# A two-layer HGRN2 and Fourier mixer block on one Trainium2 core: token mixtures rebuilt later, two heads projected plainly, sums moved to GpSimd

## The chip, the cores and the metric

The program runs on 1 core of one Trainium2 chip. The metric is device microseconds of one execution, taken as the median of several runs. The kernel before has 1232.58 us (three runs: 1232.63, 1232.58 and 1231.08). The engines are named as in the profile: PE multiplies matrices (PEld loads its weights), DVE is VectorE, ACT is ScalarE, POOL is GpSimd, and SP issues the DMAs.

## What is computed

Two layers work on 512 latent tokens of width 1024, in float32; 256 context tokens are a prefix of layer 0. Cut to what matters:

```
layer 0: h = rms_norm(x) * (1 + scale) + shift      # scale, shift, gate: adaLN of c and c_ctx
         p = h @ hg_w_in                            # 5 streams: q, f1, f2, v, z; 16 heads of 128
         f = lb + (1 - lb) * sigmoid(p[1:3])        # two gates, forward and backward scan
         o = scan_forward(q, 1 - f1, v) + scan_backward(q, 1 - f2, v)
         x = x + gate * ((rms_norm(o) * silu(z)) @ hg_w_out)
layer 1: u, z = split(h1 @ ft_w_in);  y = real(fft2(u))
         x = x + gate * ((y * silu(z)) @ ft_w_out)
out:     rms_norm(x)
```

The context tokens need the gates f1, f2 and v only (they give the state from which the latent scans start). So q and z are products over 512 tokens, f1, f2 and v over 768.

## The kernel before

Every float32 product is made from halves. `split` (lines 57 to 59) rounds a tile to a high part on ACT (`wh`) and takes the remainder on DVE (`wl`), and `mm3` (lines 102 to 105) adds three matmuls: high by high, low by high, high by low. The normalized tokens stand transposed in `hlh` and `hll`, high and low parts of [128, 8, 768].

**The start** (lines 347 to 428) has an order written out by hand for PE, ACT and DVE. For each of eight blocks `d` of the model width, PE makes adaLN's row for the block (`rp`, line 225) and transposes the latent tokens (`tp`, line 244); ACT copies the row out (`row`, line 227); PE turns it into columns (`mp`, line 233); DVE makes `acol` and `bcol` from them; `modulate` (from line 246) writes `hlh` on ACT and `hll` on DVE. The products of head 0 (`first`) for block d - 2 lie between. The same is then done for the context tokens (`e` = 1), in a second loop over `d`, after their sums of squares (`square`) and `normalize`.

**The seven-product trick.** From head 1 on, the two gate streams of a head are not made as two full products but from seven products of quarter-size blocks (`px`, 84 matmuls of 384 columns), in the manner of Strassen and Winograd. For this the weights of the two streams are folded (`fold_piece`, four sums of 128x512 a head, on DVE, lines 297 to 302: tile `wr`), each of the seven results is split (`wp`), and four of the seven products use token mixtures `mix` in place of tokens. `mixes` (line 261) makes the mixtures during the start: for one block it takes four sums or differences on POOL in place in `xs` (lines 273 to 276), and splits the four results into `mix`. It is called once a block for the latent tokens at d = 4 to 7, and for two blocks at a time for the context tokens at d = 5 and 7. The results of the products are combined by additions of 128x384 on DVE or POOL (line 574).

**The stage of the heads** is one generator, `projections`: a pair of heads is head 2p, the V product of the pair (`vps`, 144 matmuls of 256 columns), and head 2p + 1. At each of its yields, `advance` takes one step of the oldest scan, so PE goes back and forth between projections and scans. A scan takes seven levels; at each, PE multiplies `gp` (line 678), DVE updates `z` in two instructions (line 686) and puts `gp` into `am` under a mask (line 705), and ACT gathers `kk` from `z` (line 644) for the next level's `gp`. Behind the levels come `ktp`, `sp`, the states `st` (DVE, line 731), `op`, its squares `os` (ACT, line 744), `rstd_o` (POOL, lines 187 and 188), `os` scaled (line 748), and `otp`. At the same yields `ada_rest` (line 440) steps through the rest of adaLN: 32 tiles `ar` of 512 KB are loaded one at a time into one buffer and added up in `acc` under a scalar (DVE, line 463). Outside the start, a scheduler sets the order of each engine's instructions when the kernel is built; on the chip each engine then keeps that order.

**Weights.** `specs` lists the weight tiles in the order of use. `loaded(n)` issues the loads (SP, three raw buffers `wr`), `halves(n)` folds and splits, and `get(n)` decides how far ahead the splits are asked for:

```
        def get(self, n):
            self.halves(n + 3 if n in pieces and pieces[n] < 4 else n + 1)
            self.loaded(n + 3)
            return self.parts[n]
```

Behind the heads come the output product of layer 0 (`o0a`), layer 1 and the output; none of this is touched.

Of the kernel before, what the change touches and what calls it, by code (L numbers as in the profile page):

```python
# [19 lines left out]
TC = 256  # L20
# [12 lines left out]
def hgrn_fourier_kernel(ctx: ExitStack, tc: tile.TileContext, a):  # L33
# [14 lines left out]
    def psP(name):  # L48
        return psum("P", 4, name)
# [7 lines left out]
    def split(hi, lo, src):  # L57
        s.activation(hi, src, AF.Copy)  # L58
        v.tensor_tensor(out=lo, in0=src, in1=hi.bitcast(F32), op=ALU.subtract)  # L59

    class Weights:
# [33 lines left out]
                self.parts.append((hi, lo))  # L95

        def get(self, n):
            self.halves(n + 3 if n in pieces and pieces[n] < 4 else n + 1)
            self.loaded(n + 3)
            return self.parts[n]  # L100

# [103 lines left out]
    def square(n):  # L205
        if n < 2 or n == NT:
            for b in range(2):
                junk[b] = p0.tile([P, D], F32, tag=f"junk{b}", name=f"junk{n}_{b}")
        if n % 2:
            v.scalar_tensor_tensor(out=junk[1], in0=xs[:, n, :], scalar=1.0, in1=xs[:, n, :], op0=ALU.mult, op1=ALU.mult,  # L210
                                   accum_out=ss[:, n:n + 1])
        else:
            s.activation(junk[0], xs[:, n, :], AF.Square, accum_out=ss[:, n:n + 1])
# [44 lines left out]
        v.tensor_tensor(out=tl[d].rearrange("p (n c) -> p n c", c=P), in0=h32,  # L258
                        in1=th[d].bitcast(F32).rearrange("p (n c) -> p n c", c=P), op=ALU.subtract)

    def mixes(k0, k1, e):
        m, n0 = ((2, 0), (1, NT))[e]
        xt = xs.rearrange("p n (h k c) -> p h k n c", h=2, c=P)

        def part(kh, half, k):
            return xt[:, kh, k, n0 + half:n0 + half + 2 * m - 1:2, :]

        for t in range(4):
            if mix[t] is None:
                mix[t] = [ph.tile([P, KT // 2, N // 2], F32R, tag=f"t{2 * t + b}", name=f"mix{t}_{b}") for b in range(2)]  # L270
        for k in range(k0, k1):
            b11, b12, b21, b22 = (part(kh, half, k) for kh in range(2) for half in range(2))
            g.tensor_tensor(out=b22, in0=b22, in1=b12, op=ALU.subtract)
            g.tensor_tensor(out=b12, in0=b12, in1=b11, op=ALU.subtract)
            g.tensor_tensor(out=b11, in0=b22, in1=b11, op=ALU.add)
            g.tensor_tensor(out=b21, in0=b21, in1=b11, op=ALU.subtract)
            for t, src in ((2, b22), (0, b12), (1, b11), (3, b21)):
                c = slice(0, 2 * P) if e == 0 else slice(2 * P, 3 * P)
                hi, lo = (mix[t][b][:, k, c].rearrange("p (n c) -> p n c", c=P) for b in range(2))
                split(hi, lo, src)  # L280


    specs = []
    at = {}
# [6 lines left out]
    def fold_piece(w, j):  # L291
        p = pieces[j]
        w.loaded(j - p + 1)
        f1, f2 = w.raw[j - p], w.raw[j - p + 1]
        a11, a12, a21, a22 = f1[:, :4], f1[:, 4:], f2[:, :4], f2[:, 4:]
        if p == 2:
            v.tensor_tensor(out=a21, in0=a21, in1=a22, op=ALU.add)
            v.tensor_tensor(out=a11, in0=a21, in1=a11, op=ALU.subtract)
        elif p == 4:
            v.tensor_tensor(out=a21, in0=a22, in1=a11, op=ALU.subtract)  # L300
        elif p == 5:
            v.tensor_tensor(out=a12, in0=a12, in1=a11, op=ALU.subtract)
        return (a11, a12, a11, a21, a21, a12, a22)[p]

    def head_specs(i):
        if i == 0:
            for st in (1, 2):
                spec(("w", i, st), a["hg_w"][i, st], [P, KT, P])
        else:
            for p in range(7):  # L310
# [43 lines left out]
    with tc.manual_schedule(engines={mybir.EngineType.PE, mybir.EngineType.Activation, mybir.EngineType.DVE}):  # L354
# [14 lines left out]
        W.loaded(2)  # L369
        for d in range(5, KT):  # L370
            ada_load(d)
        for n in range(NTC):
            nc.sync.dma_start(out=xs[:, NT + n, :], in_=a["ctx"][n * P:(n + 1) * P, :])
        W.loaded(3)
        mraw = p0.tile([P, 5, P], F32, name="mraw")
        nc.sync.dma_start(out=mraw, in_=a["masks"][:, :5, :])
        keep_warm(24, "warm1")
# [7 lines left out]
        for d in range(KT):  # L385
            if d > 0:
                ada_mm(d)
            if d == 5:
                lower_bounds()
            turn(d, 0)  # L390
            if d == 0:
                keep_warm(4, "warm3")
            for j, k in todo.get(d, [(j, d - 2) for j in range(3)] if d > 3 else []):
                product(j, k)
            if d == KT - 1:
                for n in range(NT, NT + NTC):
                    square(n)
            ada_cols(d)
            modulate(d, 0)
            if d < 3:  # L400
                W.halves(d)
            if d >= KT // 2:
                mixes(d - 4, d - 3, 0)
        W.halves(3)
        for j in range(3):
            product(j, KT - 2)
        for n in range(NT, NT + NTC):
# [13 lines left out]
        for d in range(KT):  # L421
            modulate(d, 1)
            product(3, d)
            if d + 2 < KT:
                turn(d + 2, 1)
            if d in (5, 7):
                mixes(d - 5, d - 3, 1)
    st_start.close()

    grow = [pd.tile([1, D], F32, name=f"grow{j}") for j in range(2)]  # L430
# [5 lines left out]

    st_hgrn = ExitStack()
    sp = st_hgrn.enter_context(tc.tile_pool(name="sp", bufs=1))

    def ada_rest():  # L440
        todo = [(j, k) for j in range(4) for k in range(KT)]
# [10 lines left out]
        for j in (0, 1, 2, 3):  # L452
# [4 lines left out]
            for k in range(KT):  # L457
                yield
                raw = raws[j * KT + k]
                if k == 0 and j in (1, 2):  # L460
                    v.tensor_scalar(out=acc, in0=raw, scalar1=scol[:, 0, k:k + 1], scalar2=None, op0=ALU.mult)
                else:
                    v.scalar_tensor_tensor(out=acc, in0=raw, scalar=scol[:, 0, k:k + 1], in1=acc,
                                           op0=ALU.mult, op1=ALU.add)
                fetch()
            yield
            if j in (0, 3):
# [45 lines left out]
    def proj(i):  # L513
# [17 lines left out]
        if i == 0:  # L531
# [61 lines left out]
        s.activation(ff[:, 0, :], ff[:, 0, :], AF.Sigmoid)  # L593
        gate(2)
        yield None
        for st, dst in ((0, q), (3, zs)):
            wh, wl = W.get(at["w", i, st])
            pl = psP(f"pq{i}_{st}")
            yield from lat_proj(pl, wh, wl, hlh[:, :, :T], hll[:, :, :T])
            silu(pl, dst)  # L600
            if st == 0:
                yield None
            else:
                yield scan(i, ff, z4, q, zs)
# [543 lines left out]
```

## Time and profile before

| what | value |
|---|---|
| median of three runs | 1232.58 us |
| the profiled execution | 1230.89 us, span 1229.1 us |
| PE busy | 1182.0 us (96%), 7497 matmuls |
| DVE, ACT, POOL busy | 880.9 (72%), 600.6 (49%), 104.4 us (8%) |
| DMA | 126.29 MB, mean 103 GB/s |
| PE's idle time by stage | 24.5 us in the first 93 us, 22.5 us in the 1136 us after |

The page gives, for each engine, the time in which it was busy and how many instructions it ran. Views of the trace give the same by stretch (busy time of each engine between two times, and the clock that PE was granted), by group of instructions (count, busy time, mean duration, and the idle time just before them with what ended it), as a timeline, as a list of who waited for whom, and as the chain of work that ended last. PE's durations overlap, as matmuls are pipelined: how fast it works is read from start to start.

### The profile page before, as it was taken

Reading aid. Unit: us, or ns where it says so; the run is one execution under the profiler, and the core shown is the slowest. Engines: PE = TensorE matmul, PEld = TensorE weight load, DVE = VectorE, ACT = ScalarE, POOL = GpSimd, SP = SyncE. Lnnn points to the kernel's source line nnn. Section 1 sums busy time; section 2 is a strip of 40 time slices with the busy share of each in tenths; the row PEclk is TensorE's granted clock in tenths of the full one; section 3 lists DMA queues with packets and bytes.
Section 4 is the critical chain, followed back from the end, with each engine's and each line's share of the span. In section 5 each row is a group of like instructions: output and inputs, shape, how many; then the busy total and the mean of one; then the engine's idle time right before and its main releaser. Section 6 shows DMA issues by size and latency. Waiting matters only on the chain.

```text
span 1229.1 us, 19234 instructions
## 1 busy us (share of the span) xinstructions
PE 1182.0 (96%) x7497; PEld 1054.5 (86%) x7497; DVE 880.9 (72%) x1492; ACT 600.6 (49%) x1205; POOL 104.4 (8%) x138
## 2 busy tenths in 40 slices
PE   7779999999999999999999999999999999999997
PEld 5559889988988988998898999898888998888885
DVE  5479886786897787788568668759666856658554
ACT  4356563664555465456365455456557533333322
POOL 2330100100110011010010010010010000000000
PEclk9979999999999999999999999999999999999999
DMA  9312430220531431232022022117546313333221
GB/s 353 142 37 88 143 104 27 78 87 26 162 121 44 140 127 52 79 128 88 25 78 85 28 78 69 35 53 246 182 143 201 105 52 114 113 118 120 86 86 69
DMA packets 39585, 126.29 MB, mean 103 GB/s; under 512 B 4537, under 2 KB 8130, under 8 KB 39494
## 3 DMA queue, kind: packets, MB, share of 16 engines
q1 hardware_dynamic: 39494, 125.06, 30.0%
q8 instruction: 59, 0.97, 0.3%
q14 instruction: 32, 0.26, 0.1%
HBM read 119.52 MB, written 5.51 MB: 102 GB/s over the span
## 4 chain that ended last, share of the span: by engine, by line
PE 72%; DVE 12%; ACT 8%; POOL 3%; issue 3%; DMA 2%; SPq 0%; DVEq 0%; POOLq 0%; ACTq 0%
PE gp L678 5%; DVE z L686 4%; PE px L103 4%; PE px L104 4%; PE px L105 3%; PE pq L105 3%; PE pq L104 3%; PE pq L103 3%; PE vps L103 3%; PE vps L105 3%; PE vps L104 3%; PE o0a L105 2%; PE o0a L103 2%; PE o0a L104 2%; PE o1a L103 2%
## 5 line engine op out<-in xcount | busy, mean ns | idle before, releaser
L58 ACT ACTIVATE wh<-wr 128x1024 fp32r<-128x1024 f32 x110 | 116.3, 1057 | 153.7 <-issue 53.4
L686 DVE TENSOR_TENSOR z<-z,tt 128x512 f32<-128x512 f32 x192 | 130.3, 721 | 69.5 <-PE gp L678 67.9
L59 DVE TENSOR_TENSOR wl<-wr,wh 128x1024 fp32r<-128x1024 f32 x110 | 134.1, 1219 | 33.3 <-ACT wh L58 33.1
L103 PE MATMUL vps<-wh,hlh 128*128 128x256 f32 x384 | 112.8, 294 | 0.5 <-ACT ff L533 0.5
L678 PE MATMUL gp<-z,kk 128*128 128x128 f32 x768 | 107.7, 283 | 5.7 <-ACT kk L644 4.9
L678 PEld LDWEIGHTS gp<-z,kk 128*128 128x128 f32 x768 | 95.9, 192 | 18.8 <-ACT kk L644 18.0
L644 ACT ACTIVATE kk<-z 128x512 f32<-128x512 f32 x96 | 61.5, 640 | 100.0 <-DVE z L686 96.3
L105 PE MATMUL vps<-wh,hll 128*128 128x256 f32 x384 | 109.9, 286 | 0.0
L104 PE MATMUL vps<-wl,hlh 128*128 128x256 f32 x384 | 108.9, 284 | 0.0
L58 ACT ACTIVATE wp<-wr 128x512 fp32r<-128x512 f32 x105 | 65.0, 627 | 82.4 <-PE pq L104 73.5
L105 PE MATMUL pq<-hlh,wl 128*128 128x512 f32 x240 | 95.6, 398 | 0.0
L103 PE MATMUL pq<-hlh,wh 128*128 128x512 f32 x240 | 95.4, 397 | 0.0
L104 PE MATMUL pq<-hll,wh 128*128 128x512 f32 x240 | 94.4, 393 | 0.0
L574 POOL TENSOR_TENSOR ff<-u,c 128x384 f32<-128x384 f32 x30 | 45.4, 1515 | 492.5 <-ACT c L570 408.9
L59 DVE TENSOR_TENSOR wp<-wr,wp 128x512 fp32r<-128x512 f32 x105 | 71.0, 686 | 20.1 <-ACT wp L58 19.8
L103 PE MATMUL px<-mix,wp 128*128 128x384 f32 x240 | 84.4, 352 | 0.0
L104 PE MATMUL px<-mix,wp 128*128 128x384 f32 x240 | 82.1, 342 | 0.0
L105 PE MATMUL px<-mix,wp 128*128 128x384 f32 x240 | 81.3, 339 | 0.0
L103 PEld LDWEIGHTS vps<-wh,hlh 128*128 128x128 f32 x384 | 73.7, 192 | 2.8 <-issue 2.1
L104 PEld LDWEIGHTS vps<-wl,hlh 128*128 128x128 f32 x384 | 73.8, 192 | 0.7 <-issue 0.5
L105 PEld LDWEIGHTS vps<-wh,hll 128*128 128x128 f32 x384 | 73.8, 192 | 0.6 <-issue 0.6
L103 PE MATMUL px<-hlh,wp 128*128 128x384 f32 x180 | 62.3, 346 | 0.0
(286 smaller groups left out, 3095.1 us busy)
## 6 DMA issues: line engine op xcount, KB each, us to landing
wr<-hg_w SPq DMA_DIRECT2D x64, 512.0 KB, 3.6
ar<-ada_r SPq DMA_DIRECT2D x32, 512.0 KB, 3.5
wr<-ft_w SPq DMA_DIRECT2D x32, 512.0 KB, 4.1
wr<-hg_wout SPq DMA_DIRECT2D x29, 512.0 KB, 3.8
wa<-ada_a SPq DMA_DIRECT2D x16, 512.0 KB, 11.2
wr<-hg_v SPq DMA_DIRECT2D x16, 512.0 KB, 4.6
wr<-ft_wout SPq DMA_DIRECT2D x16, 512.0 KB, 3.5
yd<-y SPq DMA_DIRECT2D x13, 256.0 KB, 2.8
```

The costliest lines, as they stand in the source:

```text
L58: s.activation(hi, src, AF.Copy)
L59: v.tensor_tensor(out=lo, in0=src, in1=hi.bitcast(F32), op=ALU.subtract)
L103: pe.matmul(out, lh, rh, start=first, stop=False)
L104: pe.matmul(out, lh, rl, start=False, stop=False)
L105: pe.matmul(out, ll, rh, start=False, stop=last)
L574: eng.tensor_tensor(out=dst, in0=x, in1=y, op=ALU.add)
L644: s.activation(view(kk, 0, [[2 * h, T // (2 * h)], [h, 2], [1, h]]), view(z4, 2 * T, [[2 * h, T // (2 * h)], [T + h, 2], [1, h]]), AF.Copy)
L678: pe.matmul(gp[:, n * P:(n + 1) * P], kk[:, n * P:(n + 1) * P], view(z4, n * P, dims), start=True, stop=True)
L686: v.tensor_tensor(out=za, in0=za, in1=ta, op=ALU.mult)
```

## The change

1. `mixes` leaves the start. It becomes a generator that is stepped at each yield of `projections`, behind `advance`: for each of four blocks it adds the high and low parts back to whole tokens (two POOL additions of 128x768 from `hlh` and `hll` into `whole`), takes the four sums or differences on POOL over all 768 tokens (128x384 each), and splits the four results. The two `whole` tiles take the buffers of `ar` and `acc`, one of each.
2. Head 1 is projected plainly, as head 0's weights are: its two gate streams are 2 x 24 matmuls of 512 columns (latent) and 2 x 24 of 256 columns (context), in place of 84 of 384 columns. The pieces begin with head 2.
3. `fold_piece`'s four sums of 128x512 a head go from DVE to POOL (now for 14 heads, 56 sums, instead of 15 heads).
4. `ada_rest`: the multiplication by the scalar goes to ACT, in place in `ar`, and the addition of 128x1024 to POOL (30 additions; in two of 32 cases ACT writes `acc` itself).
5. `get` asks for pieces up to four ahead, and for one tile further ahead at other places.
6. In the start, the fourth weight tile is loaded ahead of the context tokens and split at d = 6, and the squares of the context tokens write their unused results to other buffers.

The diff, cut to its core (`blocks` is the rest of the old `proj`, under a name of its own):

```
         def get(self, n):
-            self.halves(n + 3 if n in pieces and pieces[n] < 4 else n + 1)
+            if n in pieces and pieces[n] < 5:
+                self.halves(min(n + 4, n + 6 - pieces[n]))
+            else:
+                self.halves(n + 2 if n + 2 in pieces else n + 1)
...
         if p == 2:
-            v.tensor_tensor(out=a21, in0=a21, in1=a22, op=ALU.add)
-            v.tensor_tensor(out=a11, in0=a21, in1=a11, op=ALU.subtract)
+            g.tensor_tensor(out=a21, in0=a21, in1=a22, op=ALU.add)
+            g.tensor_tensor(out=a11, in0=a21, in1=a11, op=ALU.subtract)
...
     def head_specs(i):
-        if i == 0:
+        if i < 2:
...
+        W.loaded(3)
         for n in range(NTC):
             nc.sync.dma_start(out=xs[:, NT + n, :], in_=a["ctx"][n * P:(n + 1) * P, :])
-        W.loaded(3)
...
             if d < 3:
                 W.halves(d)
-            if d >= KT // 2:
-                mixes(d - 4, d - 3, 0)
-        W.halves(3)
+            if d == 6:
+                W.halves(3)
...
-            if d in (5, 7):
-                mixes(d - 5, d - 3, 1)
...
+    def mixes():
+        for t in range(4):
+            mix[t] = [ph.tile([P, KT // 2, N // 2], F32R, tag=f"t{2 * t + b}", name=f"mix{t}_{b}") for b in range(2)]
+        for k in range(KT // 2):
+            whole = []
+            for e, tag in enumerate(("ar", "acc")):
+                t = sp.tile([P, D], F32, tag=tag, name=f"whole{k}_{e}")
+                kk = 4 * e + k
+                g.tensor_tensor(out=t[:, :N], in0=hlh[:, kk, :].bitcast(F32), in1=hll[:, kk, :].bitcast(F32), op=ALU.add)
+                w = t[:, :N].rearrange("p (n e c) -> p e n c", e=2, c=P)
+                whole += [w[:, 0], w[:, 1]]
+            b11, b12, b21, b22 = whole
+            yield
+            g.tensor_tensor(out=b22, in0=b22, in1=b12, op=ALU.subtract)
+            g.tensor_tensor(out=b12, in0=b12, in1=b11, op=ALU.subtract)
+            g.tensor_tensor(out=b11, in0=b22, in1=b11, op=ALU.add)
+            g.tensor_tensor(out=b21, in0=b21, in1=b11, op=ALU.subtract)
+            yield
+            for t, src in ((2, b22), (0, b12), (1, b11), (3, b21)):
+                split(*(mix[t][b][:, k, :].rearrange("p (n c) -> p n c", c=P) for b in range(2)), src)
+                if t in (0, 3):
+                    yield
...
                 if k == 0 and j in (1, 2):
-                    v.tensor_scalar(out=acc, in0=raw, scalar1=scol[:, 0, k:k + 1], scalar2=None, op0=ALU.mult)
+                    s.activation(acc, raw, AF.Copy, scale=scol[:, 0, k:k + 1])
                 else:
-                    v.scalar_tensor_tensor(out=acc, in0=raw, scalar=scol[:, 0, k:k + 1], in1=acc,
-                                           op0=ALU.mult, op1=ALU.add)
+                    s.activation(raw, raw, AF.Copy, scale=scol[:, 0, k:k + 1])
+                    g.tensor_tensor(out=acc, in0=raw, in1=acc, op=ALU.add)
...
+        next(mix_work, None)
         if step > 30 and step % 3 == 0:
             next(side_work, None)
```

What this does to the order of the instructions is seen at three places. The first is ACT in the start, blocks d = 4 to 6 of the latent tokens; `row` is adaLN's row, `mix` a high part of a mixture, `wz` the fourth weight tile, and the numbers at the ends of names tell buffers apart. Before:

```order
L250 ACTIVATE hlh<-tp_0_376,bcol,acol 128x512
L58 ACTIVATE mix_0_402<-xs 128x256
L58 ACTIVATE mix_0_398<-xs 128x256
L58 ACTIVATE mix_0_400<-xs 128x256
L58 ACTIVATE mix_0_404<-xs 128x256
L227 ACTIVATE row_427<-rp_418 128x256
L250 ACTIVATE hlh<-tp_0_433,bcol,acol 128x512
```

And now:

```order
L253 ACTIVATE hlh<-tp_0_376,bcol,acol 128x512
L230 ACTIVATE row_407<-rp_398 128x256
L253 ACTIVATE hlh<-tp_0_413,bcol,acol 128x512
L257 ACTIVATE xs<-tp_0_413,bcol,acol 128x4x128
L230 ACTIVATE row_444<-rp_435 128x256
L253 ACTIVATE hlh<-tp_0_446,bcol,acol 128x512
L58 ACTIVATE wz_468<-wr_172 128x1024
```

The next block's `row` stood behind four mixture splits and now stands right behind `hlh`.

The second place is DVE in the V product of the first pair, in the scan levels of head 0 (`z_0` and `am`; `tt` are the levels' small products). Before, with weight sums (`wr`), pieces (`wp`) and adaLN's sums (`acc`) between the levels:

```order
L686 TENSOR_TENSOR z_0_746<-z_0_746,tt_2_963 128x2x32x8 x2
L705 COPY_PREDICATED am_859<-masks,gp_3_990 128x512
L59 TENSOR_TENSOR wp_1098<-wr_827,wp_1098 128x512
L463 SCALAR_TENSOR_TENSOR acc_1951<-ar_2_2186,scol,acc_1951 128x1024
L686 TENSOR_TENSOR z_0_746<-z_0_746,tt_3_1000 128x2x16x16 x2
L705 COPY_PREDICATED am_859<-masks,gp_4_1033 128x512
L300 TENSOR_TENSOR wr_827<-wr_827,wr_820 128x512
```

And now, with the second block's mixture remainders (`mix_1`, from `whole`):

```order
L705 TENSOR_TENSOR z_0_642<-z_0_642,tt_2_882 128x2x32x8 x2
L724 COPY_PREDICATED am_770<-masks,gp_3_913 128x512
L59 TENSOR_TENSOR mix_1_723<-whole_1_933,mix_0_722 128x384
L726 TENSOR_TENSOR tt_6_1052<-tt_5_1014 128x8
L59 TENSOR_TENSOR mix_1_719<-whole_0_931,mix_0_718 128x384
L59 TENSOR_TENSOR mix_1_721<-whole_0_931,mix_0_720 128x384
L705 TENSOR_TENSOR z_0_642<-z_0_642,tt_3_923 128x2x16x16 x2
L724 COPY_PREDICATED am_770<-masks,gp_4_960 128x512
L59 TENSOR_TENSOR mix_1_725<-whole_1_933,mix_0_724 128x384
L59 TENSOR_TENSOR wl_1025<-wr_735,wh_1024 128x1024
L705 TENSOR_TENSOR z_0_642<-z_0_642,tt_4_970 128x2x8x32 x2
```

A level of the scan now stands behind remainders that wait for POOL's results.

The third place is POOL in the heads that follow (`ff` is a gate's addition, `rstd_o` a scan's scale). Before:

```order
L574 TENSOR_TENSOR ff_1371<-u_1399,c_1511 128x3x128 x2
L187 TENSOR_SCALAR rstd_o_1734<-oss_1729 128x4
L188 TENSOR_TENSOR rstd_o_1734<-rstd_o_1734,nhalf 128x4
L574 TENSOR_TENSOR ff_2031<-u_2059,c_2160 128x3x128
L187 TENSOR_SCALAR rstd_o_2182<-oss_2177 128x4
```

And now:

```order
L466 TENSOR_TENSOR acc_1942<-ar_5_2413,acc_1942 128x1024
L602 TENSOR_TENSOR ff_1325<-u_1354,c_1462 128x3x128 x2
L466 TENSOR_TENSOR acc_1942<-ar_6_2514,acc_1942 128x1024
L279 TENSOR_TENSOR wr_1712<-wr_1712 128x512
L466 TENSOR_TENSOR acc_1942<-ar_7_2619,acc_1942 128x1024
L190 TENSOR_SCALAR rstd_o_1685<-oss_1680 128x4
L191 TENSOR_TENSOR rstd_o_1685<-rstd_o_1685,nhalf 128x4
L280 TENSOR_TENSOR wr_1651<-wr_1712,wr_1651 128x512
L284 TENSOR_TENSOR wr_1651<-wr_1651 128x512
L282 TENSOR_TENSOR wr_1712<-wr_1712,wr_1651 128x512
```

Between the gates' additions and the scans' scales now stand weight sums and adaLN's additions. On SP's queue the loads of `ar` begin four weight tiles later than before.

More of the change, by code (lines that the diff above doesn't have):

```diff
@@ L207, in square @@
             for b in range(2):
-                junk[b] = p0.tile([P, D], F32, tag=f"junk{b}", name=f"junk{n}_{b}")
+                junk[b] = (p0 if n < NT else ph).tile([P, D], F32, tag=f"junk{b}" if n < NT else f"t{b}", name=f"junk{n}_{b}")
         if n % 2:
@@ L259, in modulate @@
                         in1=th[d].bitcast(F32).rearrange("p (n c) -> p n c", c=P), op=ALU.subtract)
[L261 to L280, printed above, removed]
     specs = []
@@ L296, in fold_piece @@
         if p == 2:
-            v.tensor_tensor(out=a21, in0=a21, in1=a22, op=ALU.add)
-            v.tensor_tensor(out=a11, in0=a21, in1=a11, op=ALU.subtract)
+            g.tensor_tensor(out=a21, in0=a21, in1=a22, op=ALU.add)
+            g.tensor_tensor(out=a11, in0=a21, in1=a11, op=ALU.subtract)
         elif p == 4:
-            v.tensor_tensor(out=a21, in0=a22, in1=a11, op=ALU.subtract)
+            g.tensor_tensor(out=a21, in0=a22, in1=a11, op=ALU.subtract)
         elif p == 5:
-            v.tensor_tensor(out=a12, in0=a12, in1=a11, op=ALU.subtract)
+            g.tensor_tensor(out=a12, in0=a12, in1=a11, op=ALU.subtract)
         return (a11, a12, a11, a21, a21, a12, a22)[p]
     def head_specs(i):
-        if i == 0:
+        if i < 2:
             for st in (1, 2):
@@ L545, in proj, with blocks @@
             return
+        if i == 1:
+            for st in (1, 2):
+                wh, wl = W.get(at["w", i, st])
+                pl = psP(f"pf{i}_{st}")
+                yield from lat_proj(pl, wh, wl, hlh[:, :, :T], hll[:, :, :T])
+                s.activation(ff[:, 2 - st, :T], pl, AF.Sigmoid)
+                yield None
+                pcx = psP(f"pfc{i}_{st}")
+                for k in range(KT):
+                    mm3(pcx[:, :TC], wh[:, k, :], wl[:, k, :], hctx[0][k], hctx[1][k], k == 0, k == KT - 1)
+                s.activation(ff[:, 2 - st, T:], pcx[:, :TC], AF.Sigmoid)
+                gate(st)
+                yield None
+        else:
+            yield from blocks(i, ff, gate)
+        for st, dst in ((0, q), (3, zs)):
+            wh, wl = W.get(at["w", i, st])
+            pl = psP(f"pq{i}_{st}")
+            yield from lat_proj(pl, wh, wl, hlh[:, :, :T], hll[:, :, :T])
+            silu(pl, dst)
+            if st == 0:
+                yield None
+            else:
+                yield scan(i, ff, z4, q, zs)
+    def blocks(i, ff, gate):
         base = at["f", i, 0]
@@ L595, in proj @@
         yield None
[L596 to L604, printed above, removed]
     def scan(i, ff, z4, q, zs):
@@ L826, in hgrn_fourier_kernel @@
     side_work = ada_rest()
+    mix_work = mixes()
     step = 0
```

## Prediction

> **What bounds the kernel now.** The page's totals (the table above) say PE, at 96% of the span. The stretches say where not (busy time of each engine, number of instructions in brackets, then granted PE clock, DMA share, GB/s):
>
> ```profile
> core 0: us, PE busy (x) PEld busy (x) DVE busy (x) ACT busy (x) POOL busy (x), PEclk, DMA share, GB/s
> 20.00:40.00 20.00, 18.07 (x126) 12.66 (x126) 8.69 (x17) 7.27 (x11) 0.00 (x0) 0.83 1.03 408
> 37.00:94.00 57.00, 39.61 (x216) 29.76 (x215) 35.94 (x74) 27.34 (x58) 23.07 (x41) 0.85 0.17 59
> 94.00:155.00 61.00, 59.97 (x426) 55.15 (x424) 53.98 (x88) 34.56 (x73) 4.01 (x4) 1.00 0.32 109
> 305.00:405.00 100.00, 97.55 (x668) 90.11 (x667) 80.98 (x134) 51.26 (x111) 8.81 (x8) 1.00 0.33 106
> 405.00:505.00 100.00, 98.67 (x665) 91.28 (x664) 80.20 (x135) 51.04 (x111) 9.01 (x8) 0.98 0.30 98
> 505.00:605.00 100.00, 97.18 (x650) 88.20 (x649) 78.48 (x131) 52.67 (x113) 8.83 (x8) 1.00 0.28 93
> 605.00:705.00 100.00, 99.19 (x684) 92.08 (x682) 72.89 (x127) 53.04 (x113) 8.29 (x8) 1.00 0.18 59
> ```
>
> From 37 to 94 PE rests 17.4 us, afterwards it works without a break. Hence PE's work counts after 94, and in 37 to 94 whatever PE waits for. The chain of waits names that (from 37.9 to 93.6, and pieces of it):
>
> ```profile
> by line: POOL xs L275 9.2%; POOL xs L274 9.0%; POOL xs L276 8.9%; POOL xs L273 8.7%; issue 8.6%; ACT hlh L250 6.1%; DVE hll L258 6.0%; DVE xs L256 5.8%; PE tp L244 5.1%; PE rp L225 3.1%; DVE xs L217 2.5%; PE mp L233 2.4%; ACT L533 2.3%; ACT
> ```
>
> ```profile
> 45.69 1.73 PE rp L225 x16
> ...
> 65.06 0.74 POOL xs L273
> ...
> 68.37 0.02 ACT mix L58
> ...
> 79.86 0.47 POOL xs L273
> ...
> 84.12 0.31 ACT mix L58
> ...
> 91.61 1.28 ACT L533
> ...
> 93.55 0.39 PE vps L103
> ```
>
> POOL's mixture sums hold 35.8% of 55.7 us, 20 us. PE's next `rp` waits for `row`, which stands on ACT behind four mixture splits.
>
> **The start without mixtures** (change 1). How long a block takes without mixtures is seen at block 4, the last that has none ahead of it, from one `rp` to the next (the timeline):
>
> ```profile
> 33.91 1.07 PE L225 MATMUL rp<-wa,spad 128*32 128x256 f32 x16
> 37.93 1.07 PE L225 MATMUL rp<-wa,spad 128*32 128x256 f32 x16
> ```
>
> A block takes 4.0 us; with mixtures 45.69 - 37.93 = 7.8. Three blocks save 3.75 each, 11.2; the last latent block's sums go with 68.37 - 65.06 = 3.3, the context's first call with 84.12 - 79.86 = 4.3, and the second, the same eight sums, with as much: 23.1. Once PE no longer waits for them it has the `pfc` products and weight splits to work through ahead of the V product, so I take 22.5: V starts at about 71 instead of 93.55, and ACT's table load (91.61) at about 64.5.
>
> **Head 1 plain** (change 2). Start to start, 384 columns take 0.17 to 0.18 us:
>
> ```profile
> 170.42 0.34 PE L104 MATMUL px<-mix,wp 128*128 128x384 f32 x1
> 170.60 0.33 PE L105 MATMUL px<-mix,wp 128*128 128x384 f32 x1
> ```
>
> That is 0.45 ns a column. Plain: 48 x 512 + 48 x 256 = 36,864 columns; now 84 x 384 = 32,256; so 4,608 more, **+2.1 us of PE**. If nothing but PE counted up to head 2 (155.05, below), the gain were 22.5 - 2.1 = 20.4.
>
> **The mixtures in their new place.** They must now end before head 2's first mixture product, in scans of head 0 that wait for DVE themselves. POOL's price for two sizes is in the chain above: 0.47 for 128 columns (79.86), 0.74 for 256 (65.06). Two timelines add 384 columns with DVE at rest, and the same sum beside DVE:
>
> ```profile
> 327.82 1.00 POOL L574 TENSOR_TENSOR ff<-u,c 128x384 f32<-128x384 f32 x1 [36.71 <-DVE st L731]
> ```
>
> ```profile
> 169.13 1.21 DVE L59 TENSOR_TENSOR wl<-wr,wh 128x1024 fp32r<-128x1024 f32 x1
> 169.29 1.93 POOL L574 TENSOR_TENSOR ff<-u,c 128x384 f32<-128x384 f32 x1 [4.14 <-DVE u L574]
> 170.26 2.10 DVE L686 TENSOR_TENSOR z<-z,tt 128x512 f32<-128x512 f32 x2
> ```
>
> 128, 256 and 384 columns: 0.47, 0.74, 1.00, so 0.27 for each further 128, and by that line (estimates) 1.27 for 512, 1.8 for 768, 2.4 for 1024. A block's sums are 2 x 1.8 + 4 x 1.0 = 7.6 us of POOL, four blocks 30. The last three rows, one stretch of DVE and POOL, show the two engines taking turns: POOL's sum began 0.16 behind `wl`, ended 1.0 behind `wl`'s end, and `z`'s pair took 2.10, where two alone take 1.4 (0.7 each, below). So POOL and DVE times add up wherever DVE adds two tiles.
>
> Head 0's first `z` comes 11.5 us behind the table load (91.61, and 103.09 here):
>
> ```profile
> 103.09 1.29 DVE L686 TENSOR_TENSOR z<-z,ff 128x512 f32<-128x512 f32 x2
> ```
>
> ```profile
> 135.00 0.28 ACT L744 ACTIVATE os<-op 128x128 f32<-128x128 f32 x1 [2.79 <-PE op L740]
> ```
>
> ```profile
> 155.05 0.37 PE px L103
> ```
>
> So at 76, with some 2 us of turns at 78. The first block's last remainder stands two scan levels behind it, 85.5. `whole` has one buffer each, so each further block is a loop: POOL's sums 7.6, ACT's splits, DVE's remainders, with a level of the scan between. I take 11, 15 and 12 us (7.6 of POOL, and DVE's own 3.5 to 7 in turns): the last remainder at about 124, behind which `st`, then `op`: `os` at 127.4. From `os` to head 2's first `px` (155.05) are 20.05 now, and 0.6 more: 148.05, **7 us earlier**. So of 20.4, 13 are given back, as waits of PE at `gp` and `sp`. At the ends: no turns, -20.4; loops of 15 each and a block more of turns, +1.
>
> The clock in 37 to 94 was 0.85 with 17 us of PE at rest. Rests of that kind now lie in V and head 1, where the clock was 1.00; I charge +1. The Trainium skill (TensorE: Matmul & The Clock Gate, What's actually happening) says that after an idle window of some 3.4 us PE runs at half clock until a busy window: two long rests would make it some +3.5 there instead. The 0.85 beside those rests agrees.
>
> **Weight sums and adaLN on POOL** (changes 3, 4). Groups of before, and two waits:
>
> ```profile
> L463 DVE SCALAR_TENSOR_TENSOR acc<-ar,scol,acc 128x1024 f32<-128x1024 f32 x30 | 40.0, 1333 | 14.1 <-DMA ar<-ada_r 13.8
> L298 DVE TENSOR_TENSOR wr<-wr,wr 128x512 f32<-128x512 f32 x15 | 10.3, 686 | 0.2
> L59 DVE TENSOR_TENSOR wl<-wr,wh 128x1024 fp32r<-128x1024 f32 x110 | 134.1, 1219 | 33.3 <-ACT wh L58 33.1
> L59 DVE TENSOR_TENSOR wp<-wr,wp 128x512 fp32r<-128x512 f32 x105 | 71.0, 686 | 20.1 <-ACT wp L58 19.8
> L686 DVE TENSOR_TENSOR z<-z,tt 128x512 f32<-128x512 f32 x192 | 130.3, 721 | 69.5 <-PE gp L678 67.9 <-ACT ff L589 1.0 <-ACT st L634 0.3
> ```
>
> ```profile
> L58 ACT ACTIVATE wh<-wr 128x1024 fp32r<-128x1024 f32 x110 | 116.3, 1057 | 153.7 <-issue 53.4 <-PE px L105 27.4 <-PE zp L104 26.4
> ```
>
> ```profile
> ACT os L748 <- POOL rstd_o L188: 19.5, 16, 1.7
> ```
>
> DVE loses 40 + 56 x 0.69 = 79 us. POOL gains 30 x 2.4 + 56 x 1.27 = 143. ACT gains 32 x 1.06 = 34, and has half its time free. DVE's turns cost it something again: equal when DVE wants two tiles in 79/143 = 55% of the time. By the rows it does so for 134 + 71 + 130 us and smaller ones in some 700, about half, so nearly nothing is left. What could be had at best is PE's rests with adaLN against the stretch without: (99.19 - 97.55) + (99.19 - 98.67) + (99.19 - 97.18) = 4.2 us. I take -1. The wait for `ar`'s DMA (13.8) moves from DVE to ACT, whose queue holds `kk` and the splits; `rstd_o` and the gates' additions now queue on POOL behind 2.4 us sums, and `os` (19.5 us waited already) and the scan's start behind those. Scans lie a product ahead, so I charge nothing; if that cover goes, each head loses up to 2.4.
>
> **At nothing** (5, 6): the fourth weight tile ahead of the context tokens delays them by 512 KB at 408 GB/s, 1.3 us, long before they are used; the junk buffers end a wait that the chain doesn't have. Pieces four ahead hide POOL's slower weight sums behind seven products of 2.1 us; uncovered, a late piece costs its sum and split, 1.27 + 0.63.
>
> **The sum**: -7 + 1 - 1 = -7 against the profiled execution's 1230.89, and that is 1.7 below the median; the same -7 from the median, 1232.58, gives **1225.5**.
>
> **The rivals.** *B, the mixtures are hidden*: DVE's turns are short, PE alone counts to head 2: -20.4, and -4.2 of adaLN's waits: 1208. For it: PE has products enough in the stage. Against it: DVE was busy 54 of 61 there without the mixtures.
>
> *C, POOL's sums hold up DVE in the heads*, slower. If DVE wants two tiles always, it gains 143 - 79 = 64 us over 650, 10 per 100 where 19 to 22 are free. PE waits for `z` through `kk`; if a third of it reaches PE, +21, less the start's 7: 1232.6 + 21 - 7 = 1246. It decides above 55%. Against it: my count of a half. For it: POOL has no buffer to run ahead in. The Trainium skill (Perfetto Trace Analysis, Optimizing Scalar/DVE Operations) says that GpSimd and DVE share a read port of SBUF, so that moving work between the two might not help; the rows at 169.13 agree.
>
> *D, all is given back in V and head 1*: three loops of 15 us, 45 in place of 38, are +7 against the -7: 1232.6, no change. For it: the second block is reckoned at 15 already, having a whole scan level between its remainders.
>
> **How the numbers follow.** A, the forecast, .45, its own range 1218 to 1234; B .25; C .18; D .12. A difference of 0.2% (2.5 us) is about what a measurement of this kernel can tell. Faster: A .33, B .25: .58. Same: A .08, D .08: .16. Slower: A .04, C .18, D .04: .26. The range takes in B's centre and nearly C's: 1206 to 1245.
>
> **What the new profile would show.** Right: no POOL on the chain before 65; V at 70 to 72; PE rests of some 13 us between 71 and 148, ended by `z`, `kk` or `st`; POOL's four sums at 1.0 where DVE is idle and near 2 beside it; mean of `z` above 0.72; head 2's `px` near 148. Wrong: `px` near 135 (B), or past 155 (D); PE's stretches 305 to 605 clearly under 97 of 100 with `z` and `wl` stretched (C); POOL's 768-column sums far from 1.8 would change every loop.

## The result and the profile after

The changed kernel takes **1284.17 us** (median of four runs, 1283.28 to 1286.39) against 1232.61 for the kernel before: a ratio of 1.0423, 95% interval 1.0405 to 1.0441. It is 51.6 us slower, where 7 us faster was forecast. The profiled execution has a span of 1281.5 us. Line numbers from here on are those of the changed kernel.

First the start, where the forecast can be read directly. The timeline of the changed kernel shows ACT's table load, the first matmul of the V product, and the first product of head 2:

```profile
63.55 1.28 ACT L535 ACT_TABLE_LOAD   x1 [1.37 <-DVE hll L261]
...
68.56 0.28 PE L106 MATMUL vps<-wh,hlh 128*128 128x256 f32 x1
...
146.06 0.33 PE L106 MATMUL px<-hlh,wp 128*128 128x384 f32 x1
```

For the kernel before, the prediction took 155.05 as head 2's first `px`. The timeline of that kernel has it earlier: the 84 `px` of head 1 end at 141.4, and the first of the next 84 is this one:

```profile
152.21 0.33 PE L103 MATMUL px<-hlh,wp 128*128 128x384 f32 x1
```

(The row at 155.05 stands behind twelve of them and the scan's `cs`.) V starts at 68.6 instead of 93.55, and head 2 at 146.06 instead of 152.21: 25 us gained in the start, 19 of them given back up to head 2, 6 left. The loss lies behind that, nearly 58 us. The stretches of the changed kernel, with the columns as before:

```profile
core 0: us, PE busy (x) PEld busy (x) DVE busy (x) ACT busy (x) POOL busy (x), PEclk, DMA share, GB/s
37.00:94.00 57.00, 48.06 (x354) 41.44 (x354) 44.65 (x72) 28.76 (x52) 21.28 (x20) 0.98 0.20 65
94.00:155.00 61.00, 49.04 (x285) 43.09 (x285) 46.56 (x54) 30.22 (x62) 37.66 (x24) 0.94 0.25 73
305.00:405.00 100.00, 88.46 (x545) 80.48 (x544) 68.38 (x99) 53.94 (x100) 33.37 (x19) 0.95 0.30 93
405.00:505.00 100.00, 90.68 (x602) 83.92 (x601) 65.67 (x100) 51.93 (x103) 36.42 (x22) 0.95 0.29 95
505.00:605.00 100.00, 88.67 (x585) 80.48 (x583) 68.56 (x105) 51.78 (x110) 37.10 (x22) 0.97 0.26 82
605.00:705.00 100.00, 97.22 (x652) 88.80 (x653) 68.87 (x115) 51.19 (x112) 19.70 (x16) 1.00 0.18 57
```

In the three stretches with adaLN PE now rests 9 to 12 of 100 us (1 to 3 before), and it is granted 0.95 to 0.97 of its clock (0.98 to 1.00 before). In 605 to 705, where POOL makes weight sums only, it rests 2.8 (0.8 before). DVE is less busy in these four stretches than before (66 to 69 of 100 us, 73 to 81 before), and ACT has nearly half its time free. So no engine became the bound by its busy time.

What the scans wait for is in the chain of waits, here from 134 to 166:

```profile
134.09 2.41 POOL acc L466
136.51 4.02 DMA ar<-ada_r
140.62 1.17 ACT ar L465
141.85 2.57 POOL acc L466
144.44 3.62 DMA ar<-ada_r
148.14 1.16 ACT ar L465
149.36 3.05 POOL acc L466
...
164.31 0.86 issue
165.17 0.62 ACT kk L663
165.84 1.17 PE gp L697 x8
```

That is a ring of four: POOL adds a tile, the one buffer `ar` is loaded again, ACT scales it, POOL adds; a round takes 7.5 to 8 us. At its end stands `kk`, which PE waits for and which stood on ACT's queue behind the scaling. At this place that costs PE only 0.23 us. One level earlier another cause costs it more, as the timeline of the same stretch shows:

```profile
157.31 2.38 POOL L466 TENSOR_TENSOR acc<-ar,acc 128x1024 f32<-128x1024 f32 x1 [4.91 <-ACT ar L465]
157.46 3.38 DVE L705 TENSOR_TENSOR z<-z,tt 128x512 f32<-128x512 f32 x2
...
161.56 1.16 PE L697 MATMUL gp<-z,kk 128*128 128x128 f32 x8 [1.46 <-ACT kk L663]
```

Beside POOL's addition the pair of `z` takes 3.38 us (1.28 five us later, with POOL at rest), and PE rests 1.46 for the `kk` behind it. At the end of a scan the queues of ACT and POOL come in as well, in the timeline of the changed kernel (`os` are the squares, then their scaling; `otp` is PE's transpose):

```profile
340.05 1.15 ACT L465 ACTIVATE ar<-ar,scol 128x1024 f32<-128x1024 f32 x1 [2.79 <-DMA ar<-ada_r]
341.10 0.26 ACT L763 ACTIVATE os<-op 128x128 f32<-128x128 f32 x1
...
341.28 3.27 POOL L466 TENSOR_TENSOR acc<-ar,acc 128x1024 f32<-128x1024 f32 x1 [3.89 <-DMA wr<-hg_w]
...
344.51 1.26 POOL L279 TENSOR_TENSOR wr<-wr 128x512 f32<-128x512 f32 x1
...
346.13 1.02 POOL L191 TENSOR_TENSOR rstd_o<-rstd_o,nhalf 128x4 f32<-128x4 f32 x1
...
347.60 1.25 PE L771 MATMUL otp<-ident,os 128*128 128x128 f32 x4 [4.97 <-ACT os L767]
```

Three things stand in a row: ACT waits 2.79 us for the load with the squares behind it; POOL adds for 3.27 us (2.4 when alone) and sums weights for 1.26, with `rstd_o` behind both; PE rests 4.97 us. What follows is read from the clock, in short stretches of the same kernel:

```profile
341.50:347.50 6.00, 1.13 (x7) 0.80 (x5) 1.40 (x2) 1.05 (x8) 5.83 (x5) 1.00 0.32 101
347.50:350.90 3.40, 3.30 (x12) 3.08 (x13) 1.00 (x2) 3.40 (x8) 2.07 (x2) 0.51 0.44 177
350.90:354.30 3.40, 3.40 (x17) 2.96 (x16) 3.13 (x4) 2.89 (x5) 1.13 (x2) 0.99 0.52 154
```

For 3.4 us behind the rest PE has half its clock, so that a rest of 5 us costs up to 1.7 more (an estimate: half of 3.4).

That leaves three suspects, and the runs are about their shares: the **ring** (one buffer, a round of some 7.7 us in place of 4.9 to 5.6 before, where DVE's additions start at 312.86, 317.72, 323.22 and 328.83), the **queues** of ACT and POOL (what stands behind the moved sums), and the **port** (POOL's sums hold up DVE's). The last shows in two groups, POOL's additions and the scans' `z` on DVE (721 ns before):

```profile
L466 POOL TENSOR_TENSOR acc<-ar,acc 128x1024 f32<-128x1024 f32 x30 | 78.1, 2605 | 92.6 <-ACT ar L465 83.2 <-DMA acc<-brow 5.5 <-DMA wr<-hg_w 3.9
```

```profile
L705 DVE TENSOR_TENSOR z<-z,tt 128x512 f32<-128x512 f32 x192 | 154.1, 843 | 92.6 <-PE gp L697 88.7 <-ACT wp L58 2.1 <-ACT ff L617 1.0
```

### The profile page after: what moved, and what is told of

Same layout as the page of the kernel before. It is cut to its first block, busy times and chain, and to the rows that moved or that the text cites. A ratio compares the mean times of both kernels' runs of the same rounds, so it can differ in the third digit from the quotient of the medians.

```text
span 1281.5 us, 19295 instructions
## 1 busy us (share of the span) xinstructions
PE 1193.1 (93%) x7509; PEld 1061.4 (83%) x7509; DVE 877.5 (68%) x1374; ACT 624.2 (49%) x1216; POOL 275.4 (21%) x214
## 4 chain that ended last, share of the span: by engine, by line
PE 59%; DVE 15%; ACT 8%; issue 7%; POOL 5%; DMA 4%; SPq 0%; DVEq 0%; POOLq 0%; ACTq 0%
DVE z L705 4%; PE gp L697 4%; PE pq L108 3%; POOL acc L466 2%; PE vps L106 2%; PE pq L107 2%; PE pq L106 2%; PE vps L108 2%; PE vps L107 2%; PE o0a L108 2%; PE o0a L106 2%; PE o0a L107 2%; PE px L106 2%; PE px L107 2%; DMA ar<-ada_r 2%
## 5 line engine op out<-in xcount | busy, mean ns | idle before, releaser
L705 DVE TENSOR_TENSOR z<-z,tt 128x512 f32<-128x512 f32 x192 | 154.1, 843 | 92.6 <-PE gp L697 88.7
L59 DVE TENSOR_TENSOR wl<-wr,wh 128x1024 fp32r<-128x1024 f32 x112 | 139.3, 1244 | 35.8 <-ACT wh L58 35.4
L466 POOL TENSOR_TENSOR acc<-ar,acc 128x1024 f32<-128x1024 f32 x30 | 78.1, 2605 | 92.6 <-ACT ar L465 83.2
L58 ACT ACTIVATE wp<-wr 128x512 fp32r<-128x512 f32 x98 | 60.5, 625 | 66.1 <-PE pq L107 59.6
L59 DVE TENSOR_TENSOR wp<-wr,wp 128x512 fp32r<-128x512 f32 x98 | 74.9, 776 | 25.6 <-ACT wp L58 25.5
L106 PE MATMUL px<-mix,wp 128*128 128x384 f32 x224 | 82.3, 368 | 0.0
L107 PE MATMUL px<-mix,wp 128*128 128x384 f32 x224 | 79.5, 355 | 0.0
L108 PE MATMUL px<-mix,wp 128*128 128x384 f32 x224 | 78.8, 352 | 0.0
L602 POOL TENSOR_TENSOR ff<-u,c 128x384 f32<-128x384 f32 x28 | 39.1, 1397 | 143.6 <-ACT c L598 126.0
```

Of the source, the lines that this page charges most:

```text
L106: pe.matmul(out, lh, rh, start=first, stop=False)
L107: pe.matmul(out, lh, rl, start=False, stop=False)
L108: pe.matmul(out, ll, rh, start=False, stop=last)
L466: g.tensor_tensor(out=acc, in0=raw, in1=acc, op=ALU.add)
L602: eng.tensor_tensor(out=dst, in0=x, in1=y, op=ALU.add)
L705: v.tensor_tensor(out=za, in0=za, in1=ta, op=ALU.mult)
```

## The experiments

Each edit is against the changed kernel unless said otherwise. The kernel before, run beside each set, had 1231.88, 1230.56, 1230.81 and 1229.78 us.

**1. Which of the moved sums: adaLN's, the weights', or both.** In the first run adaLN's sums go back:

```diff
-                    s.activation(raw, raw, AF.Copy, scale=scol[:, 0, k:k + 1])
-                    g.tensor_tensor(out=acc, in0=raw, in1=acc, op=ALU.add)
+                    v.scalar_tensor_tensor(out=acc, in0=raw, scalar=scol[:, 0, k:k + 1], in1=acc,
+                                           op0=ALU.mult, op1=ALU.add)
```

In the second the weight sums do (the four of `fold_piece`), in the third both:

```diff
-            g.tensor_tensor(out=a21, in0=a21, in1=a22, op=ALU.add)
+            v.tensor_tensor(out=a21, in0=a21, in1=a22, op=ALU.add)
...
```

> The changed kernel (1284.17 us) with adaLN's sums as before: one DVE instruction a tile, nothing of it on ACT and GpSimd; weight sums stay on GpSimd. In the changed kernel the four stretches in which adaLN's tiles are summed lose 53.4 us, the others 8.2 us, and the way to head 2 gains 8.9 us. Ring theory (one buffer for a tile of adaLN: load, ACT, GpSimd, next load, 7.7 us a round instead of 5.0, and ACT and GpSimd stand still in it with the scan's work behind them): all of the 53 comes back, about 1231 us. Port theory (GpSimd's sums hold up DVE, in proportion to their time: adaLN's 78 us, weight sums 81 us): half of the 62 comes back, about 1253 us.

> The changed kernel with the weight sums back on DVE, adaLN's sums stay on ACT and GpSimd. Ring theory: the ring is untouched, only the 8 us come back, about 1276 us (some more if GpSimd's queue is shorter for adaLN's additions, 1270). Port theory: half of the loss comes back, about 1253 us.

> Both of these: what is left of the change are the mixtures out of the start, head 1 plain, pieces four ahead. Both theories: the loss of 62 us goes, the gain of 8.9 up to head 2 stays: about 1223 us. If this kernel is not clearly faster than before, the start's gain is given back later for a reason that neither theory has.

(The 8.9 us up to head 2 count from 155.05; from its first product they are 6.) Measured: adaLN back 1246.65 us (ratio 1.0122, 1.0102 to 1.0142), weight sums back 1268.09 (1.0294, 1.0274 to 1.0314), both back **1224.38** (0.9941, 0.9921 to 0.9961). From the last one up, the weight sums on POOL cost 22.3 us, adaLN's sums 43.7, both 59.8. Neither theory hit the first two: 37.5 came back where the one said 53 and the other 31, and 16 where they said 8 to 14 and 31. The two costs measured one at a time add up to 66, more than the 59.8 together, so they overlap. The third came out as expected: what is left of the change is 7.5 us faster than before, clear of no change.

How a weight sum costs PE time with POOL's queue empty is seen in one place, the timeline of the run with adaLN back on DVE (`wr` is the weight sum, `wp` the piece's split):

```profile
725.68 2.39 DVE L705 TENSOR_TENSOR z<-z,tt 128x512 f32<-128x512 f32 x2
725.84 1.67 POOL L282 TENSOR_TENSOR wr<-wr,wr 128x512 f32<-128x512 f32 x1 [16.47 <-DVE wp L59]
...
727.55 0.63 ACT L58 ACTIVATE wp<-wr 128x512 fp32r<-128x512 f32 x1 [0.60 <-POOL wr L282]
...
728.16 0.63 ACT L663 ACTIVATE kk<-z 128x512 f32<-128x512 f32 x1
```

And the same place with all sums on DVE:

```profile
705.57 0.69 DVE L282 TENSOR_TENSOR wr<-wr,wr 128x512 f32<-128x512 f32 x1
...
706.18 1.28 DVE L705 TENSOR_TENSOR z<-z,tt 128x512 f32<-128x512 f32 x2
...
707.55 0.63 ACT L663 ACTIVATE kk<-z 128x512 f32<-128x512 f32 x1 [0.18 <-DVE z L705]
```

One remainder on DVE releases the weight sum and lets `z` start, in the same moment. On DVE the sum took 0.69 and `z` followed in 1.28; on POOL the sum took 1.67 and `z` 2.39. What DVE was relieved of it waited for, with the next `gp` behind it: `kk` starts 2.5 us behind the start of these rows, and 2.0 with the sum on DVE.

This isn't the only way. In the same run with adaLN back on DVE, ACT waits 21.4 us in all for the weight sum of line 282, with other work behind it on its queue, and three of these waits are long. The middle of one:

```profile
351.51 3.77 POOL L282 TENSOR_TENSOR wr<-wr,wr 128x512 f32<-128x512 f32 x1 [5.74 <-DVE wp L59]
...
355.31 0.63 ACT L58 ACTIVATE wp<-wr 128x512 fp32r<-128x512 f32 x1 [4.61 <-POOL wr L282]
...
356.74 0.68 ACT L663 ACTIVATE kk<-z 128x512 f32<-128x512 f32 x1
...
357.48 1.62 PE L697 MATMUL gp<-z,kk 128*128 128x128 f32 x8 [1.97 <-ACT kk L663]
```

Here POOL's sum is the one that is stretched, to 3.77 us beside DVE's work, and `kk` stands on ACT's queue behind the piece that waits for it. So the port and ACT's queue are both in the weight sums' 22.3 us, and no run parts them.

**2. The ring cut by halves.** Tiles of 512 columns with three buffers for adaLN (loads, scaling and additions by halves):

```diff
+                for h in range(2):
+                    t = sp.tile([P, 512], F32, tag=f"ar{(2 * len(raws) + h) % 3}", name=f"ar{j}_{k}_{h}")
...
```

> The changed kernel with the ring cut: adaLN's tiles are loaded, scaled on ACT and added on GpSimd in halves of 512 columns with three buffers, so that loads run beside the sums; the work of ACT and GpSimd stays (60 additions of 512 columns in place of 30 of 1024). One of the mixtures' whole tiles is made in two halves. Ring theory: 30 to 50 us come back, 1234 to 1254 us. Port theory: GpSimd's time is the same or more, so 1284 us or slower.

1272.21 us (1.0327, 1.0307 to 1.0347): 12 us back where the ring theory asked for 30 to 50 and the port theory for none. But ACT still waited 33.9 us for loads (41.7 before the cut), so this cut the ring only in part, and it decides little.

**3. Ring, ACT and POOL one by one**, all with weight sums on DVE. The first and the last have adaLN's sums on DVE as well, the other two are edits of the run with only adaLN's sums moved: spare additions on POOL that nobody reads; a second tile for adaLN's loads (in buffers of `y13` and `y14`, empty until the last heads); ACT's scaling with the addition on DVE; and two tiles with all on DVE. The edits, in this order:

```diff
+                    for h in range(2):
+                        spare = sp.tile([P, 512], F32, tag="spare", name=f"spare{j}_{k}_{h}")
+                        g.tensor_tensor(out=spare, in0=hlh[:, k, :512].bitcast(F32), in1=hll[:, k, :512].bitcast(F32), op=ALU.add)
```

```diff
+                        raw = py.tile([P, 512], F32, tag=f"y{13 + h}", name=f"ar{j}_{k}_{h}")
...
+        fetch()
         fetch()
```

```diff
-                    g.tensor_tensor(out=acc, in0=raw, in1=acc, op=ALU.add)
+                    v.tensor_tensor(out=acc, in0=raw, in1=acc, op=ALU.add)
```

> All sums on DVE as in the run with both on DVE (1224.38 us), and beside each of adaLN's 30 additions GpSimd makes two additions of 128x512 from the normalized tokens into a spare tile that nobody reads: GpSimd's time (some 76 us) and its hold on the port as in the changed kernel, but no ring and no queue that anybody waits for, except rstd_o and the gates' additions behind them on GpSimd. Ring theory: no change, 1224 to 1228 us. Port theory: as the run with only adaLN's sums on GpSimd, 1268 us. Half by half: about 1246 us.

> The run with only adaLN's sums moved (1268.09 us), with a second tile for adaLN's loads, in buffers that stand empty until the last pair of heads; every second tile is made in two halves. Loads then run a whole tile ahead, so that the round of 7.5 us falls to about half, below the 5.0 of before. Ring theory: nearly all of the 44 us comes back, 1224 to 1232 us. Port theory: 1268 us. Half by half: about 1246 us.

> The same run with the scaling on ACT and one tile, but the addition on DVE: the ring is load 3.7 + ACT 1.15 + DVE 1.2, 6.1 us a round against 5.0 with one DVE instruction and 7.5 with GpSimd; no GpSimd. Ring theory: 1.1 of 2.5 of the 44 us stays, 1243 us. Port theory: 1224 us. Half by half: about 1234 us.

> A version meant to beat both: all sums on DVE (1224.38 us), and adaLN's loads with two tiles, so that DVE's 15 us of waits for them go. If a third to a half of those reach PE: 1217 to 1221 us. If none, 1224 us.

The spare sums gave 1289.54 us, and the run tells nothing of the question: since they depend on nothing, all 60 were ordered ahead of the mixtures, and all of the loss lies before head 2 (which starts at 211.7 us, at 143.8 without them). Two tiles: 1259.9 (1.0229, 1.0203 to 1.0254), 8.2 less than with one; ACT's waits for the loads fell from 36.3 to 19.5 us, so the ring isn't wholly gone. ACT's scaling with the addition on DVE: **1222.95** (0.9942, 0.9920 to 0.9964), no slower than with one DVE instruction, though its ring is longer than that of before. Two tiles with all on DVE: 1224.38, nothing. So a ring theory by itself falls: without POOL a ring of some 6 us (load, scaling and addition) costs nothing, and with POOL and half of the waits for loads gone 35.5 of the 43.7 are left.

**4. Port or queue.** The spare sums again, each tied to adaLN's step by one column that DVE writes; the run with two tiles with `rstd_o` and the gates' additions moved from POOL to DVE (where `rstd_o` is a product in place of a power, so that the output isn't the reference's); and the spare sums replaced by fills of about the same time:

```diff
+                    tok = sp.tile([P, 1], F32, tag="tok", name=f"tok{j}_{k}", bufs=4)
+                    v.tensor_copy(tok, acc[:, 0:1])
+                    for h in range(2):
+                        spare = sp.tile([P, 448], F32, tag="spare", name=f"spare{j}_{k}_{h}")
+                        g.tensor_copy(spare[:, 0:1], tok)
+                        g.tensor_tensor(out=spare, in0=hlh[:, k, :448].bitcast(F32), in1=hll[:, k, :448].bitcast(F32), op=ALU.add)
```

```diff
-        add(g, out(1, 1), tri(u), tri(c5))
+        add(v, out(1, 1), tri(u), tri(c5))
...
```

```diff
-                        g.tensor_tensor(out=spare, in0=hlh[:, k, :448].bitcast(F32), in1=hll[:, k, :448].bitcast(F32), op=ALU.add)
+                        for _ in range(3):
+                            g.memset(spare, 0.0)
```

> The spare sums again, now in their place: all sums on DVE (1224.38 us), and after each of adaLN's sums GpSimd first copies one column that DVE wrote behind it, then makes two additions of 128x448 from the normalized tokens into a spare tile (about 68 us in all), twice. Nobody reads them; only rstd_o and the gates' additions stand behind them. Port or queue on GpSimd (no ring): 25 to 35 us slower than 1224.38, 1250 to 1260 us, as with two tiles (1259.9 us). If only ring and ACT's queue counted: 1225 to 1228 us.

> The run with two tiles (1259.9 us), where nothing stands behind adaLN's additions on GpSimd any more: rstd_o and the gates' additions go to DVE (16 x 2 small ones, 28 of 128x384). [...] If GpSimd's queue is the cost, 20 to 30 us come back: 1230 to 1240 us. If the port is: 1255 us or slower, since DVE has 15 us more.

> As the spare sums in place, but with fills (no tile is read): three fills of 128x448 for each addition, about 80 us of GpSimd. Queue theory: as slow as the spare sums in place, 1250 to 1260 us. Port theory, if only sums that read from SBUF hold DVE up: 1225 to 1235 us; if writes hold it too, as slow as the sums.

Spare sums in place: 1254.69 us (1.0197, 1.0182 to 1.0213), **30.3 slower** than without them. Fills: 1231.92 (1.0006, 0.9996 to 1.0016), **7.5 slower**. The two stand at the same steps and keep POOL for about the same time, as POOL's groups show, sums then fills (with the copies of one column ahead of them 118 and 108 us):

```profile
L472 POOL TENSOR_TENSOR spare<-hlh,hll 128x448 f32<-128x448 f32 x60 | 84.9, 1414 | 4.8
```

```profile
L473 POOL MEMSET spare<- 128x448 f32 x180 | 85.1, 473 | 10.1
```

DVE's `z` in the two runs, again sums then fills:

```profile
L711 DVE TENSOR_TENSOR z<-z,tt 128x512 f32<-128x512 f32 x192 | 144.7, 794 | 61.4 <-PE gp L703 60.6 <-ACT st L659 0.3
```

```profile
L712 DVE TENSOR_TENSOR z<-z,tt 128x512 f32<-128x512 f32 x192 | 135.9, 749 | 64.2 <-PE gp L704 63.0 <-ACT st L660 0.7
```

Sums stretch `z` to 794 ns, fills leave it at 749 (752 with no spare work at all). DVE as a whole is busy for 914.6 us with sums and for 883.9 both with fills and without spare work. `os` waits for `rstd_o` 34.1 us with sums, 32.6 with fills, and 20.9 without spare work, so POOL's queue is as long in both. Hence 22.8 of the 30.3 us are the port, and some 7.5 are POOL's queue. The short queue gave 1247.63 us (1.0139, 1.0123 to 1.0154), 12.3 less than with two tiles, though DVE has 15 us more to do. It lies between the two expectations. But it doesn't part the two causes: the 28 gates' additions that left POOL are sums of two tiles as well, and `z`'s mean fell from 828 to 793 ns, so that some of the 12.3 may be the port. The Trainium skill (SBUF — State Buffer, Who interferes with whom) says that a DVE instruction with two inputs from SBUF contends with a GpSimd instruction that reads SBUF, and not with one that only writes it; the sums (794 ns) and the fills (749) agree.

**5. The stage of V and head 1.** From V to head 2's first product it takes 75.2 us in the kernel with ACT's scaling and DVE's additions (1222.95), 58.7 before (93.55 to 152.21; the 13.4 us of the expectations count to 155.05). Three edits of that kernel: a second set of `whole` tiles; the mixtures' sums on DVE; the sums left out, so that the splits read the tokens' high parts. The first two edits:

```diff
+                        t = py.tile([P, 512], F32, tag=f"y{13 + n}", name=f"whole{k}_{n}") if n < 3 else \
+                            sp.tile([P, N // 2], F32, tag="spare", name=f"whole{k}_{n}")
...
```

```diff
-                g.tensor_tensor(out=t[:, :N], in0=hlh[:, kk, :].bitcast(F32), in1=hll[:, kk, :].bitcast(F32), op=ALU.add)
+                v.tensor_tensor(out=t[:, :N], in0=hlh[:, kk, :].bitcast(F32), in1=hll[:, kk, :].bitcast(F32), op=ALU.add)
...
-            g.tensor_tensor(out=b22, in0=b22, in1=b12, op=ALU.subtract)
+            v.tensor_tensor(out=b22, in0=b22, in1=b12, op=ALU.subtract)
...
```

> A version meant to beat both: weight sums on DVE, adaLN scaled on ACT and added on DVE (1222.95 us), and the mixtures' whole tiles twice, the second set in four tiles that are empty at this time, so that a block's sums do not wait for the remainders of the one before. From V to head 2's first product this stage takes 13.4 us longer than before; if the loop through one buffer is its cause, half to all of that comes back: 1210 to 1216 us. If turns with DVE are its cause: 1221 to 1224 us.

> Weight sums on DVE, adaLN scaled on ACT and added on DVE (1222.95 us), and now the mixtures' sums on DVE too, in their new place: 4 x (2 of 128x768 + 4 of 128x384), by DVE's own prices (1.22 for 1024 columns, 0.55 for 384) about 4 x 4.1 = 16 us of DVE and no GpSimd between V and head 2. If turns with GpSimd make that stage long (13.4 us over before): 1215 to 1219 us. If DVE's work in it does: 1225 to 1235 us.

> The same kernel with the mixtures' sums left out: the splits read the high parts of the tokens, so that the mixtures and the output are not the reference's, but the splits and all later work stay. What the sums cost where they now stand, whoever makes them: if the stage is long because of the sums, V to head 2 falls by 10 to 13 us and the time to 1210 to 1214 us; if it is long because of the splits and of scans that wait for DVE, it falls by under 4 us.

The second set gave 1225.33 us (0.9959, 0.9945 to 0.9974), no gain, and 78.1 us from V to head 2: the loop through one buffer, on which the prediction had built this stage, is not what makes it long. Sums on DVE: **1207.69 us** (0.9816, 0.9795 to 0.9837), 15.3 less, beyond what was expected. Sums left out: 1209.54 (0.9835, 0.9817 to 0.9854), the same within a measurement. From V to head 2 it takes 58.9 us with the sums on DVE and 60.0 with none, about as long as before. So the sums on DVE cost nothing there that can be measured, and on POOL all of the stage's loss. The stretch from V to head 2 with the sums on POOL, and then on DVE:

```profile
69.00:144.30 75.30, 62.66 (x413) 56.63 (x413) 64.36 (x83) 37.94 (x78) 34.50 (x24) 0.95 0.21 67
```

```profile
69.00:128.00 59.00, 58.67 (x414) 53.61 (x413) 55.59 (x99) 34.69 (x76) 1.65 (x2) 1.00 0.19 64
```

DVE runs 99 instructions in place of 83 and is busy for 9 us less, in a stretch that is 16 us shorter: its own sums take 0.55 us for 384 columns and 0.94 for 768, where POOL takes 1.1 to 1.6 and 2.1 and holds up others meanwhile (DVE's remainders `mix` take 0.55 us in place of 0.72). PE works through, at its full clock, and head 2 starts at 128.0 instead of 144.3.

## Why the prediction was wrong

The start came out: V at 68.6 (71 said), the table load at 63.55 (64.5). The prediction's row for head 2 was misread, since 155.05 is its thirteenth `px`; from the first, at 152.21, head 2 starts 6 us earlier where 7 were said. The gain in the start was 2.5 us larger than said and what was given back some 3 larger (19 against 15.5), so that the two errors offset; that the sum came so close is partly luck. The run that keeps just this part is at 1224.38 us, and the sum's -7 + 1 gives 1226.6 for it. The price in V and head 1 was about right as a size, and only half as a cause: turns between POOL and DVE, yes (15.3 us), the loop through one buffer, no.

The step that failed is **"I take -1" for the weight sums and adaLN on POOL**. It measured +60 (1284.17 against 1224.38 with these sums back on DVE). Three things in it:

- *"Nearly nothing is left"*: DVE's balance was right. Its busy time is 877.5 us, against 883.9 with the sums back on it (880.9 before): of 79 us taken off, turns gave back all but 6. But the balance of an engine that isn't the bound was the wrong measure. DVE had 19 to 22 of 100 us free in adaLN's stretches before, and PE waits for `z`, not for DVE's total. A POOL sum that starts with a `z` adds its time to that level of the scan: `gp`, `z`, `kk` and the next `gp` wait for each other. The pair of runs with sums and fills measured 22.8 us for stand-ins of adaLN's additions, which makes this some half of adaLN's 43.7. The weight sums' 22.3 us were not taken apart: the place at 725 shows this cause, the one at 351 ACT's queue behind a stretched sum.
- *"Scans lie a product ahead, so I charge nothing; if that cover goes, each head loses up to 2.4"*: the cover went. `os` waits for `rstd_o` behind POOL's sums, PE rests up to 5 us at `otp` (13.1 us in all, 0.7 before). The runs put 7.5 us (fills) to at most 12.3 us (short queue) on POOL's queue.
- *"The wait for `ar`'s DMA moves to ACT"*, at no price: the wait grew from 13.8 to 41.7 us, as the ring became longer. A second tile, which took about half of the wait away, gives back 8.2.

Taken away in this order, the second tile (8.2) and the short queue (12.3) leave 23.2 of the 43.7, near the 22.8 by sums against fills. That isn't a proof of the shares: the 23.2 is merely what is left, the short queue also took sums off the port, and each share depends on the order. Shown are the 59.8 for the moved sums, and that the port has a large part in adaLN's; the exact shares stay open. The price of a rest itself was under-sized: the clock was charged +1, for V and head 1 alone, and in 305 to 605 it lacks 5 + 5 + 3 of 300 us (0.95, 0.95, 0.97), where it lacked 2 before. That isn't a cause of its own: it goes with the rests.

Of the rivals, C was right in kind and too small. It took a third of what DVE would gain in net work, above a share of 55%; DVE's net work came out below nothing (-6.4 us), and 60 us were lost all the same. Of its sign, `z` and `wl` stretched, only `z` came clearly (721 to 843 ns; `wl` 1219 to 1244). B's place, the mixtures hidden, is where 1207.69 us came out (1208 said), but by moving the sums to DVE, not by leaving them on POOL, so the same number is luck. One reading was slightly off, without effect: in the rows at 169.13 POOL's sum ended 0.88 us behind `wl`, not 1.0.

## What to carry to other kernels

Work that was taken off an engine with time to spare bought nothing here, and it cost where it landed, as the new engine shares a port with the old one: ask not whether the sum of both fits, but which dependent instruction the moved one will run beside. A moved instruction brings its waits into its new queue, so list what stands behind it there. Before a port or a buffer is blamed, a pair of spare loads that differ in that alone (sums against fills here) tells them apart in two runs.

## What the runs showed of the hardware

A sum of two SBUF tiles on POOL and one on DVE hold each other up; fills of the same total time don't (`z` 794 ns with sums, 749 with fills, 752 with neither; 30.3 against 7.5 us of the kernel's time). After a rest of some 5 us PE has half its clock for 3.4 us (0.51 in 347.5 to 350.9), and the full clock then (0.99 in the next 3.4). The Trainium skill (TensorE: Matmul & The Clock Gate, What's actually happening) says that PE falls to half its clock after an idle window of some 3.4 us and comes back after a busy one, and the trace agrees. DVE's price for a sum of 768 columns out of SBUF was 0.94 us where nothing held it up, against 2.05 on POOL in the changed kernel.
